# The token part of a decoder layer's projection: plain x against scaled weights, in a front written out as one fixed order

## The chip, the cores and the metric

The kernel runs on one core of a Trainium2 chip. The metric is device time: microseconds (us) from start to end of one execution of the program. Five engines work side by side, each from its own instruction queue: PE (TensorE, the matmuls), ACT (ScalarE), DVE (VectorE), POOL (GpSimd) and SP (SyncE, which here only issues DMAs). They meet at semaphores.

## The reference, cut to what matters

One layer of a decoder trunk for 1024 prompt tokens of one request and 8 x 8 = 64 tokens of eight sample requests, D = 1024, all in float32:

```python
def rms_norm(x, g):
    y = xf * lax.rsqrt(jnp.mean(xf * xf, axis=-1, keepdims=True) + EPS)
    return (y * g.astype(jnp.float32)).astype(x.dtype)
...
mod = (jax.nn.silu(c) @ w_ada + b_ada)[:, None, :]
shift1, scale1, gate1, shift2, scale2, gate2 = jnp.split(mod, 6, axis=-1)
h = rms_norm(x, norm1) * (1 + scale1) + shift1
z = h @ w_in
(q, kc, vc, ks, vs, kw, vw, gates, conv_bg, conv_cg, conv_h, pool_in) = jnp.split(z, IN_SPLITS, axis=-1)
```

`c` differs by request: the prompt has one row of `shift1` and `scale1`, each of the eight sample requests has its own. Then follow attention of three kinds, a short convolution, a pooling, the output projection and a SwiGLU; the change touches none of them. The change concerns `h`, and the 280 columns of `z` that are wanted with the tokens as rows: `vs`, `vw` (128 columns each) and `gates` (24).

## The kernel before, in words

Everything up to `h` is called the front here. Tokens lie in three **chunks** of columns, `CHUNKS = [(0, 384), (384, 384), (768, 320)]`; the last 64 columns of chunk 2 are the sample tokens. A chunk is a tile of 128 partitions x 8 k-tiles x columns, with the channels on the partitions. Chunk 0 is loaded into `x0`, chunk 1 into the memory of `kv`, chunk 2 into `x2`. SP's queue carries x of chunk 0, 16 tiles `wada` of 256 KB (modulation round 1, the scale), x of chunk 1, two halves of the token weights `wtok`, 16 more `wada` (round 0, the shift), x of chunk 2, `w1` of the compression, and then twelve blocks `cacheA`.

- **Modulation** (`ada_rounds`): 16 tiles of weights by the 32 columns of `sc` = silu(c) fill a PSUM bank; ACT copies it out (`ada_s`), PE transposes it (L145), DVE adds the bias (`mod`, L397), and after round 1 forms `s1` = (1 + scale1) * norm1 (L404).
- **Norm** (`norm_scale`): ACT squares x by k-tile (`n_t`, L441), PE multiplies `mean_d` by each square (8 float32 matmuls of 384 columns for each of the chunks 0 and 1; for chunk 2 DVE adds the squares into `n_ss` and one matmul follows), ACT takes the root, DVE the reciprocal of all 384 columns (L448), so `n_rs` holds 1/rms of each token on all partitions.
- **h** (`modulate`): DVE multiplies x by s1 and `n_rs` in place (L468), ACT adds the shift and rounds to the matmul's type (`h_hi`, L475), DVE forms the rest (`h_lo`, L477). Products are made of three matmuls (`mm3`): hi by hi, hi by lo, lo by hi.
- **Token part** (`token_part`): the 280-column weights are split into `wt_hi` (ACT) and `wt_lo` (POOL). For each of nine tiles of 128 tokens, 24 matmuls: the tile of h is stationary, 280 columns of weights move (8 k-tiles x 3 products). ACT or DVE copies the bank into `vt` and `gates`, and POOL's queue stores it. The ninth tile overlaps the eighth and holds the sample tokens. After the sixth (`tok_last`) the compression may begin.
- **Projections**: then `input_projection` multiplies the other column tiles of w_in (kc, vc, cg0, ch0, ...) with weights as the stationary side and h moving, chunk by chunk (24 matmuls of 384 or 320 columns each). Tile kc needs `w_hi`, `w_lo` (128 x 1024, ACT and DVE) and the h of all three chunks.

All of this is written as generators (`front`, `token_part`, `compress`, `first_ahead`, `late_ada`) that a small scheduler interleaves by estimated engine times; what stands in an engine's queue runs in that order. Matmuls all go through one helper, line L141, and so have one line.

## Time and profile before

| | |
|---|---|
| median of 3 runs | 1627.37 us (1626.49 to 1627.93) |
| the profiled execution's own time | 1627.8 us |
| its span | 1626.2 us |
| PE busy | 1554.4 us (96%), 12569 matmuls |
| DVE, ACT, POOL busy | 1026.3, 720.5, 591.8 us |
| mean granted TensorE clock | 0.983 |

The span lies between the first and the last instruction; 1.6 us of the time lie outside it. Busy time counts matmuls, vector and scalar operations, not the issue of DMAs. The idle time before an instruction is put down to what released it last. A PE row of the timeline gives the start, the time to the modelled end of the last matmul in it, the shapes, the count, and the idle time ahead of it. Matmuls overlap, so the price of one in a run is the distance of successive starts, not its duration. Float32 matmuls leave two records for each instruction.

### The profile page before, as it was taken

The numbers are of one execution on the slowest core, as the hardware profiler recorded it, in microseconds if no ns is written. First come the engines' busy times: TensorE is split into PE (matmuls) and PEld (weight loads), VectorE is DVE, ScalarE is ACT, GpSimd is POOL, SyncE is SP. The second block draws the span as 40 slices with busy tenths as digits, with TensorE's granted clock in tenths as the row PEclk, the third lists the DMA queues.
The fourth block names the chain that finished last, engine by engine and source line by source line (L and its number), as shares of the span: only waits on it lengthen the run. The fifth ranks groups of instructions, "written<-read, shape, count | busy, mean of one in ns | idle before, by whom it ended". The sixth has DMA issues, their size and how long they took to land.

```text
span 1626.2 us, 34746 instructions
## 1 busy us (share of the span) xinstructions
PE 1554.4 (96%) x12569; PEld 1378.6 (85%) x12569; DVE 1026.3 (63%) x2474; ACT 720.5 (44%) x1654; POOL 591.8 (36%) x715
## 2 busy tenths in 40 slices
PE   6899999996899999999899999999999999999999
PEld 2899997895776666556599999999999999999999
DVE  4723224896465577756589878776777776257462
ACT  3522215444576776765657544433334334223220
POOL 3241110166333222322212366544454444276140
PEclk9999999998999999999999999999999999999999
DMA  9486655454565575234287775446333445999872
GB/s 339 173 290 195 197 173 165 147 182 148 176 188 158 155 207 181 81 120 138 90 309 235 262 253 182 149 143 211 137 140 141 149 149 189 322 395 345 285 237 85
DMA packets 197597, 318.06 MB, mean 196 GB/s; under 512 B 26353, under 2 KB 130354, under 8 KB 197106
## 3 DMA queue, kind: packets, MB, share of 16 engines
q1 hardware_dynamic: 174930, 277.15, 51.1%
q0 software_dynamic: 9568, 28.40, 5.3%
q10 hardware_dynamic: 12928, 10.29, 2.0%
q8 instruction: 100, 1.64, 0.4%
q14 instruction: 71, 0.58, 0.1%
HBM read 245.75 MB, written 74.20 MB: 197 GB/s over the span
## 4 chain that ended last, share of the span: by engine, by line
PE 44%; DVE 5%; DMA 3%; ACT 3%; issue 3%; POOL 2%; SPq 0%; ACTq 0%; POOLq 0%; DVEq 0%
PE bank L141 43%; ACT P L1148 2%; DMA w_raw<-in_wup 1%; PE bank L145 1%; DVE P L1136 1%; DVE w_lo L173 1%; DMA pair<-mix_d 1%; POOL b_t L173 0%; DVE b_lo L173 0%; ACT w_hi L177 0%; DMA x_d<-x1a 0%; POOL pair L1779 0%; POOL f_T L173 0%; DMA w_raw<-in_wout 0%; DVE co L1458 0%
## 5 line engine op out<-in xcount | busy, mean ns | idle before, releaser
L141 PE MATMUL bank<-b_lo,w_hi 128*128 128x272 f32 x1232 | 352.8, 288 | 1.0 <-DVE b_lo L173 1.0
L141 PE MATMUL bank<-b_hi,w_hi 128*128 128x272 f32 x1232 | 350.5, 289 | 2.4 <-ACT f_m L1752 1.0
L141 PE MATMUL bank<-b_hi,w_lo 128*128 128x272 f32 x1232 | 347.4, 288 | 0.0
L141 PEld LDWEIGHTS bank<-b_hi,w_hi 128*128 128x128 f32 x1232 | 229.8, 188 | 4.9 <-ACT f_m L1752 2.8
L141 PEld LDWEIGHTS bank<-b_lo,w_hi 128*128 128x128 f32 x1232 | 231.6, 188 | 2.0 <-DVE b_lo L173 1.9
L141 PEld LDWEIGHTS bank<-b_hi,w_lo 128*128 128x128 f32 x1232 | 229.5, 188 | 0.0
L1158 POOL TENSOR_SCALAR P<-P,st 128x128 f32<-128x128 f32 (+10 forms) x192 | 108.4, 578 | 227.5 <-DVE st L1154 150.0
L173 DVE TENSOR_TENSOR w_lo<-w_raw,w_hi 128x512 fp32r<-128x512 f32 (+1 forms) x111 | 102.7, 935 | 72.8 <-ACT w_hi L177 72.2
L141 PEld LDWEIGHTS bank<-stream 128*128 128x128 f32 x1056 | 127.2, 198 | 18.1 <-issue 11.3
L141 PE MATMUL bank<-stream 128*128 128x128 f32 x1056 | 133.4, 284 | 7.1 <-DMA stream<-in_cacheA 7.0
L1148 ACT ACTIVATE P<-P,st 128x128 f32<-128x128 f32 (+10 forms) x192 | 112.7, 588 | 52.3 <-DVE st L1136 33.5
L141 PE MATMUL bank<-h_hi,w_hi 128*128 128x384 f32 (+1 forms) x384 | 130.7, 340 | 0.5 <-DVE q L769 0.5
L177 ACT ACTIVATE w_hi<-w_raw 128x512 fp32r<-128x512 f32 (+1 forms) x113 | 75.7, 687 | 123.9 <-PE bank L141 90.4
L141 PE MATMUL bank<-h_hi,w_lo 128*128 128x384 f32 (+1 forms) x384 | 126.3, 329 | 0.0
L141 PE MATMUL bank<-h_lo,w_hi 128*128 128x384 f32 (+1 forms) x384 | 125.6, 327 | 0.0
L173 DVE TENSOR_TENSOR w_lo<-w_s,w_hi 128x512 fp32r<-128x512 f32 x110 | 111.1, 1010 | 15.7 <-ACT w_hi L177 13.1
L141 PE MATMUL bank<-g,w_hi 128*128 128x272 f32 x608 | 114.6, 288 | 0.0
L1779 POOL TENSOR_TENSOR pair<-pair,f_v 128x272 f32<-128x272 f32 x44 | 44.5, 1012 | 186.2 <-DVE f_v L1749 145.5
L173 POOL TENSOR_TENSOR w_s<-w_raw 128x512 f32<-128x512 f32 x60 | 88.4, 1474 | 44.5 <-DVE w_lo L173 42.1
L141 PEld LDWEIGHTS bank<-g,w_hi 128*128 128x128 f32 x608 | 94.9, 188 | 0.0
L177 ACT ACTIVATE w_hi<-w_s 128x512 fp32r<-128x512 f32 x110 | 69.0, 628 | 52.6 <-PE bank L141 30.5
L141 PE MATMUL bank<-g,w_lo 128*128 128x272 f32 x304 | 86.4, 287 | 0.0
(399 smaller groups left out, 3694.6 us busy)
## 6 DMA issues: line engine op xcount, KB each, us to landing
g<-g_d SPq DMA_DIRECT2D x42, 816.0 KB, 6.7
g_d<-f_s SPq DMA_DIRECT2D x57, 544.0 KB, 3.4
wada<-in_wada SPq DMA_DIRECT2D x96, 256.0 KB, 5.2
stream<-in_cacheA SPq DMA_DIRECT2D x192, 128.0 KB, 3.2
unit<-in_cacheB SPq DMA_DIRECT2D x152, 128.0 KB, 2.3
w_raw<-in_wup SPq DMA_DIRECT2D x38, 512.0 KB, 4.3
stream<-in_cacheB SPq DMA_DIRECT2D x104, 128.0 KB, 2.2
w_raw<-in_wout SPq DMA_DIRECT2D x24, 512.0 KB, 5.0
```

Source lines behind the costliest of these rows:

```text
L141: return self.nc.tensor.matmul(out, lhsT, rhs, start=start, stop=stop, skip_group_check=chain)
L145: return self.nc.tensor.transpose(out, in_, self.ident if ident is None else ident)
L173: (self.nc.vector if eng == "dve" else self.nc.gpsimd).tensor_tensor(out, a, b, op=op)
L177: self.last_hi = self.nc.scalar.activation(hi, src, AF.Copy)
L1136: self.last_evac = nc.vector.tensor_tensor_reduce(out=Pt[:, 2 * g + hl, col:col + n], in0=S[g][:, p0:p0 + n], in1=mk, scale=-1.0, scalar=3 ...
L1148: nc.scalar.activation(Ps, Ps, AF.Exp, scale=-1.0, bias=sy[:, g, 0:1], accum_out=sy[:, g, 1:2])
L1158: nc.gpsimd.tensor_scalar(Ps, Ps, sy[:, g, 3:4], 0.0, op0=OP.mult, op1=OP.add)
L1779: nc.gpsimd.tensor_tensor(g[:, 1], s1, v, op=OP.mult)
```

## The change: what it does

Algebra: with r = 1/rms of a token (a row of the token part's result) and s, sh per channel, (x * r * s + sh) @ w = r * (x @ (s * w)) + sh @ w. In the kernel after,

- the token weights are multiplied by s1 (`w[0]` on ACT, `w[1]` on DVE) and x is split without any scaling (`hi`, `lo`); eight token tiles multiply these; ACT applies r when it copies the bank out (`out`), as a number for each partition. The term sh @ w comes from 8 matmuls of 32 columns over the raw weights, a mean matmul, and is added to `vt` and `gates` at the very end of the front, on DVE;
- the sum of squares is added up on DVE, one matmul of a single column for each 128 tokens gives the mean square with the tokens on the partitions (`sums`), the reciprocal is taken of three numbers a partition, and three matmuls by the identity lay it out over the columns again (`spread`) for the final h;
- the sample tokens go another way: x of these 64 columns is scaled and shifted on DVE and multiplied by the raw weights in 8 float32 matmuls with 64 stationary columns;
- the final h (`scaled`, `hi2`, `lo2`) is formed behind: chunk 0 among the last token tiles, chunk 1 after the first `yield`, chunk 2 after the second. The split of kc's weights stands between chunk 0 and chunk 1, that of vc's between 1 and 2;
- everything in the front is issued through `ordered`, which chains the instructions of each engine in the order of the code. `wada` has 12 buffers instead of 16; the last four tiles of round 0 are asked for after the matmuls `ada(4)`. On SP's queue `w1`, kc's and vc's raw weights (which take over the buffers of `wada`) and four `wada` of a later round (in the memory of `x0`) follow, and only then the blocks `cacheA`.

```diff
+    def front(self, h, np_, ap, tp):
...
+        def sums(c):
+            m = self.bank()
+            for q, a in enumerate(starts(c)):
+                M(m[:, q:q + 1], ss[:, a:a + P], self.mean_d[:, 0:1], True, True)
+            A(rt[c], m[:, 0:3], AF.Sqrt, bias=self.eps[:, 0:1])
+            V("reciprocal", rt[c], rt[c])
+            b = np_.tile([P, 384], F32, name="n_rb")
+            V("tensor_copy", b.rearrange("p (q m) -> p q m", q=3), rt[c][:, :, None].to_broadcast([P, 3, P]))
+            return b
...
+        def scaled(c, k):
+            n = size[c]
+            V("scalar_tensor_tensor", x[c][:, k, :n], x[c][:, k, :n], s[:, k, 0:1], rs[c][:, :n], op0=OP.mult, op1=OP.mult)
...
+        def out(j, acc):
+            r = rt[j // 3][:, j % 3:j % 3 + 1]
+            A(self.vt[:, j, 0:256], acc[:, 0:256], AF.Copy, scale=r)
+            A(self.gates[:, j, :], acc[:, 256:280], AF.Copy, scale=r)
...
+        for k in range(KT):
+            square(0, k)
+            hi(0, k)
+            lo(0, k)
...
+        b = sums(0)
+        ada(3, acc)
+        t = ada_rows(acc)
+        ada_turn(t, 1)
...
+        for k in range(KT):
+            A(w[0][:, k], raw[k // 4][:, k % 4], AF.Copy, scale=s[:, k, 0:1])
+            V("scalar_tensor_tensor", w[1][:, k], raw[k // 4][:, k % 4], s[:, k, 0:1], w[0][:, k].bitcast(F32),
+              op0=OP.mult, op1=OP.subtract)
+        spread(0, b)
+        t0 = token(0)
...
+        t3 = token(3)
+        b = sums(1)
+        ss = self.pair384(0)
+        run(square, 2, range(8))
+        acc = self.bank()
+        ada(4, acc)
+        ada_load(7)
+        out(3, t3)
+        ada(5, acc)
+        t4 = token(4)
+        spread(1, b)
+        run(hi, 2, range(8))
+        run(lo, 2, range(8))
+        b = sums(2)
+        ada(6, acc)
+        out(4, t4)
+        ada(7, acc)
+        t = ada_rows(acc)
+        spread(2, b)
+        run(scaled, 0, range(8))
...
+        t5 = token(5)
+        self.tok_last = self.order["pe"]
+        X(self.w1, i["w1"].rearrange("p v k m -> p (v k) m"))
+        ada_turn(t, 0)
...
+        run(hi2, 0, range(8))
+        run(lo2, 0, range(8))
+        t6 = token(6)
+        m = self.bank()
+        for y in range(2):
+            for g in range(4):
+                M(m[32 * g:32 * g + 32, 0:280], sb[:, 4 * y + g], raw[y][:, g], y == 0, y == 1)
+        acc = self.bank()
+        for k in range(KT):
+            M(acc[64:128, 0:280], v[:, k], raw[k // 4][:, k % 4], k == 0, k == KT - 1)
+        t7 = token(7)
+        yield
...
+        M(m[:, 0:280], self.mean_d, part, True, True)
...
+        run(scaled, 1, range(8))
+        run(hi2, 1, range(8))
+        run(lo2, 1, range(8))
+        yield
+        run(scaled, 2, range(8))
...
+        run(hi2, 2, range(8))
+        run(lo2, 2, range(8))
+        for d, a, n in ((self.vt, 0, 256), (self.gates, 256, 24)):
+            V("scalar_tensor_tensor", d[:, 0:8], m[:, None, a:a + n].to_broadcast([P, 8, n]), float(D // 32), d[:, 0:8],
+              op0=OP.mult, op1=OP.add)
```

In `input_projection` the two `yield`s of `front` are met so:

```diff
             load()
             load()
-            split()
+            front_split()
+            next(front)
+            front_split()
+            for _ in front:
+                pass
...
+            self.spawn(0.6, self.up_weights_ahead(pp, 0))
             self.spawn(0.5, self.late_ada())
```

**PE, the start of the program.** Before: `n_t` are the squares of x, `wada,sc` the modulation, `ident,ada_s` its transposes; the first token matmul is the last row shown.

```order
L141 MATMUL bank<-n_t,mean_d 128x384 x3
L141 MATMUL bank<-wada,sc 32x256 x2
L141 MATMUL bank<-n_t,mean_d 128x384 x2
L141 MATMUL bank<-wada,sc 32x256 x6
L141 MATMUL bank<-n_t,mean_d 128x384
...
L141 MATMUL bank<-wada,sc 32x256 x22
L145 MATMUL bank<-ident,ada_s 128x128 x2
L141 MATMUL bank<-wt_hi,h_hi_103 128x280
```

After, from the first matmul on (`pair_182` is the sum of squares of chunk 0, `n_rb` the 1/rms that is laid out; `h_hi_103` holds plain x here):

```order
L141 MATMUL bank<-wada,sc 32x256 x24
L141 MATMUL bank<-mean_d,pair_182 128x1 x3
L141 MATMUL bank<-wada,sc 32x256 x8
L145 MATMUL bank<-ident,ada_s 128x128 x2
L141 MATMUL bank<-ident,n_rb 128x128 x3
L141 MATMUL bank<-wt_hi,h_hi_103 128x280
```

Both modulation rounds and the means of chunks 0 and 1 stood ahead of the first token matmul; now one round and three one-column matmuls do.

**PE, from the fifth token tile to the first projection, after.** The second modulation round, the layouts of chunks 1 and 2, and the matmuls of the shift (`ct`) and of the sample tokens (`x_153`):

```order
L141 MATMUL bank<-ident,n_rb 128x128 x3
L141 MATMUL bank<-mean_d,pair_484 128x1 x3
L141 MATMUL bank<-wada,sc 32x256 x16
L141 MATMUL bank<-ident,n_rb 128x128 x2
L141 MATMUL bank<-ident,n_rb 128x64
...
L141 MATMUL bank<-stream,ct 32x280 x8
L141 MATMUL bank<-stream,x_153 64x280 x8
...
L141 MATMUL bank<-n_t,mean_d 128x280
L141 MATMUL bank<-h_hi_103,w_hi 128x384
```

The first projection (kc, the last row) now follows the mean matmul of the shift; of the compression's matmuls (`c_peT`, `stream 128x128`), which stood among the last token tiles and ahead of kc in the kernel before, none stands ahead of it.

**DVE, the forming of h.** Before (`x_154` is chunk 0, `kv__98` chunk 1, `s_128` is s1, `h_lo_104` and `h_lo_106` the rest of h):

```order
L448 RECIPROCAL n_rs<-n_rs 128x384
L397 TENSOR_TENSOR mod<-bank,c_bada 128x4x9 x2
L404 SCALAR_TENSOR_TENSOR s_128<-mod,c_norm_113 128x72
L468 SCALAR_TENSOR_TENSOR x_154<-x_154,s_128,n_rs 128x384 x8
L448 RECIPROCAL n_rs<-n_rs 128x384
L468 SCALAR_TENSOR_TENSOR kv__98<-kv__98,s_128,n_rs 128x384 x8
L397 TENSOR_TENSOR mod<-bank,c_bada 128x4x9 x2
L477 SCALAR_TENSOR_TENSOR h_lo_104<-x_154,mod,h_hi_103 128x384 x8
```

After, from the rest of plain x of chunk 2 (`h_lo_108`) to the end of the front's work on chunk 1 (`pair_328` and `pair_563` hold 1/rms of chunks 0 and 1, laid out):

```order
L370 TENSOR_TENSOR h_lo_108<-x_153,h_hi_107 128x256 x8
L370 RECIPROCAL n_rt_156<-n_rt_156 128x3
L370 COPY n_rb<-n_rt_156 128x384
L370 SCALAR_TENSOR_TENSOR x_152<-x_152,s_128,pair_328 128x384 x8
...
L370 COPY ct<-mod 128x256
L370 TENSOR_TENSOR x_153<-x_153,mod 128x8x64
L370 SCALAR_TENSOR_TENSOR h_lo_104<-x_152,mod,h_hi_103 128x384 x8
L173 TENSOR_TENSOR w_lo<-w_raw,w_hi 128x1024
L370 SCALAR_TENSOR_TENSOR kv__98<-kv__98,s_128,pair_563 128x384 x8
L370 SCALAR_TENSOR_TENSOR h_lo_106<-kv__98,mod,h_hi_105 128x384 x8
```

The reciprocals of 384 columns are gone; the scaling of x and the forming of `h_lo` stand behind the splits of plain x, and `w_lo` of kc (L173) between chunk 0 and chunk 1.

## Rows read from the trace of the kernel before

**Rows 1.** The page's span and its row of busy times (busy us, share of the span, instructions).

```profile
span 1626.2 us, 34746 instructions
PE 1554.4 (96%) x12569; PEld 1378.6 (85%) x12569; DVE 1026.3 (63%) x2474; ACT 720.5 (44%) x1654; POOL 591.8 (36%) x715
```

**Rows 2.** The windows of core 0: from-to and length in us, then busy us (instructions) of PE, weight loads, DVE, ACT and POOL, the granted clock, the busy share of the DMA engines and GB/s.

```profile
0.00:45.00 45.00, 29.59 (x164) 10.62 (x164) 20.45 (x36) 15.33 (x27) 13.50 (x23) 1.00 0.97 346
45.00:58.20 13.20, 10.29 (x74) 9.87 (x75) 12.06 (x26) 11.42 (x26) 1.62 (x3) 0.95 0.53 166
58.20:88.60 30.40, 30.40 (x242) 30.20 (x241) 19.18 (x41) 12.68 (x27) 11.74 (x18) 0.96 0.52 188
88.60:118.47 29.87, 29.87 (x196) 27.69 (x194) 7.84 (x15) 8.63 (x19) 11.54 (x17) 1.00 0.80 270
...
350.00:850.00 500.00, 455.96 (x4374) 334.09 (x4373) 327.41 (x1291) 314.42 (x842) 163.97 (x288) 0.95 0.53 162
...
0.00:10.00 10.00, 0.00 (x0) 0.00 (x0) 0.55 (x6) 2.13 (x3) 6.32 (x17) 1.00 0.76 235
10.00:20.00 10.00, 9.86 (x42) 3.27 (x42) 1.09 (x6) 2.60 (x6) 0.00 (x0) 1.00 1.05 380
```

**Rows 3.** The three longest waits of PE up to 90 us: what was waited for, us in total, times, the longest.

```profile
PE bank L141 <- ACT n_t L441: 10.4, 2, 10.1
PE bank L141 <- DVE n_ss L173: 2.9, 1, 2.9
PE bank L141 <- ACT h_hi L475: 2.3, 1, 2.3
```

**Rows 4.** The timeline of PE, from the last token tile to the second projection's end (start, us, engine, line, matmul, shapes, count). At 88.60 kc begins, at 118.47 cg0.

```profile
79.08 3.63 PE L141 MATMUL bank<-c_peT,stream 128*128 128x2 f32 x32
82.57 6.27 PE L141 MATMUL bank<-stream 128*128 128x128 f32 x54
88.60 0.42 PE L141 MATMUL bank<-h_hi,w_hi 128*128 128x384 f32 x1
...
118.47 0.42 PE L141 MATMUL bank<-h_hi,w_hi 128*128 128x384 f32 x1
```

**Rows 5.** The loads at the start: SP's issue of the 16 `wada` of round 1, and ACT's first work on x, with its wait.

```profile
2.10 13.66 SPq L368 DMA_DIRECT2D wada<-in_wada  x16
...
9.57 0.52 ACT L441 ACTIVATE n_t<-x 128x384 f32<-128x384 f32 x1 [5.99 <-DMA x<-in_xT]
```

**Rows 6.** The timelines of ACT and DVE: the split of kc's weights (`w_hi`, `w_lo`), the forming of s1 (`s<-mod`), and the scaling of chunk 2's 256 prompt columns.

```profile
28.23 2.60 DVE L404 SCALAR_TENSOR_TENSOR s<-mod,c_norm 128x72 f32<-128x72 f32 x1
...
62.27 3.25 DVE L468 SCALAR_TENSOR_TENSOR x<-x,s,n_rs 128x256 f32<-128x256 f32 x8
...
78.54 1.04 ACT L177 ACTIVATE w_hi<-w_raw 128x1024 fp32r<-128x1024 f32 x1
...
79.61 1.23 DVE L173 TENSOR_TENSOR w_lo<-w_raw,w_hi 128x1024 fp32r<-128x1024 f32 x1
```

**Rows 7.** The timeline of PE at the front: modulation matmuls, transposes, and the token matmuls at either clock.

```profile
10.14 1.65 PE L141 MATMUL bank<-n_t,mean_d 128*128 128x384 f32 x2 [10.14 <-ACT n_t L441]
...
17.47 0.91 PE L141 MATMUL bank<-n_t,mean_d 128*128 128x384 f32 x2
...
26.71 1.56 PE L141 MATMUL bank<-n_t,mean_d 128*128 128x384 f32 x4
...
36.10 1.93 PE L141 MATMUL bank<-wada,sc 128*32 128x256 f32 x30
...
45.01 0.40 PE L141 MATMUL bank<-wt_hi,h_hi 128*128 128x280 f32 x1 [2.31 <-ACT h_hi L475]
...
57.44 1.43 PE L141 MATMUL bank<-n_ss,mean_d 128*128 128x320 f32 x2 [2.90 <-DVE n_ss L173]
...
58.90 0.43 PE L141 MATMUL bank<-wt_lo,h_hi 128*128 128x280 f32 x1
59.13 0.43 PE L141 MATMUL bank<-wt_hi,h_lo 128*128 128x280 f32 x1
...
60.48 0.29 PE L141 MATMUL bank<-wt_hi,h_lo 128*128 128x280 f32 x1
...
60.99 0.29 PE L141 MATMUL bank<-wt_hi,h_hi 128*128 128x280 f32 x1
```

**Rows 8.** Page, DMA issues: KB each and median us from issue to landing.

```profile
wada<-in_wada SPq DMA_DIRECT2D x96, 256.0 KB, 5.2
stream<-in_cacheA SPq DMA_DIRECT2D x192, 128.0 KB, 3.2
```

**Rows 9.** Groups by shape over the whole span (busy us, mean ns of one, idle before): the nearest form to the sample matmuls (64 stationary columns).

```profile
L141 PE MATMUL bank<-pair,c_w 64*64 64x256 f32 x64 | 7.7, 433 | 3.9 <-ACT pair L625 3.9
```

**Rows 10.** The timeline of DVE: the scaling of chunk 0, eight operations that begin while POOL works on the token weights, and the same eight of chunk 1.

```profile
30.86 6.51 DVE L468 SCALAR_TENSOR_TENSOR x<-x,s,n_rs 128x384 f32<-128x384 f32 x8
...
39.88 4.32 DVE L468 SCALAR_TENSOR_TENSOR kv__98<-kv__98,s,n_rs 128x384 f32<-128x384 f32 x8
```

**Rows 11.** The timeline of POOL: the two operations of the token weights, then issues of DMAs.

```profile
28.18 5.09 POOL L173 TENSOR_TENSOR wt_lo<-stream,wt_hi 128x1120 fp32r<-128x1120 f32 x2 [18.85 <-ACT wt_hi L177]
33.21 2.15 POOL L533 DMA_DIRECT2D stream<-in_cacheA  x4
```

**Rows 12.** The waits of PE over the whole span: the blocks of the compression.

```profile
PE bank L141 <- DMA stream<-in_cacheA: 7.0, 3, 5.0
```

More of the change, by code (lines that the diff above doesn't have):

```diff
@@ L546, in compress @@
         yield from self.hold(lambda: self.tok_last)
-        if self.w1 is None:
+        if not self.compressing:
+            self.compressing = True
+            yield from self.hold(lambda: self.w_load)
             yield from self.compress_setup(pool)
@@ L683, in load @@
             if i < len(srcs):
+                if i == 0:
+                    st["hi"] = pool.tile([P, D], F32R, name="w_hi", bufs=bufs)
                 t = pool.tile([P, D], F32, name="w_raw", bufs=raw_bufs)
-                nc.sync.dma_start(t, srcs[i])
+                load_ = nc.sync.dma_start(t, srcs[i])
+                if i < 2:
+                    self.w_load = load_
                 st["raw"][i] = (t, self.use("dma", 1.45, self.t["pe"]) + 2.0)
@@ L694, in split @@
                 t, at = st["raw"].pop(i)
-                hi = pool.tile([P, D], F32R, name="w_hi", bufs=bufs)
+                hi = st["hi"] if i == 0 else pool.tile([P, D], F32R, name="w_hi", bufs=bufs)
                 lo = pool.tile([P, D], F32R, name="w_lo", bufs=bufs)
@@ L716, in project @@
         return acc[:, :n]
-    def token_loads(self):
-        for half in range(2):
-            raw = self.stream_tile().rearrange("p a b -> p (a b)")[:, 0:1120].rearrange("p (k m) -> p k m", k=4)
-            self.nc.sync.dma_start(raw, self.i["wtok"][:, half * 4:half * 4 + 4])
-            self.wt_raw.append((raw, self.use("dma", 1.5, self.t["pe"]) + 2.0))
-    def token_part(self, pool, h):
-        nc = self.nc
-        hi = pool.tile([P, KT, 280], F32R, name="wt_hi")
-        lo = pool.tile([P, KT, 280], F32R, name="wt_lo")
-        yield from self.hold(lambda: self.wt_raw)
-        for half, (raw, at) in enumerate(self.wt_raw):
-            s = slice(half * 4, half * 4 + 4)
-            yield at
-            r = self.split(hi[:, s], lo[:, s], raw, 1120, at, "pool")
-        yield r
-        for j in range(9):
-            c0 = j * P if j < 8 else T - P
-            ch = next(k for k, (a, n) in enumerate(CHUNKS) if a <= c0 and c0 + P <= a + n)
-            yield from self.hold(lambda: ch in self.h_done)
-            yield max(self.h_at[ch])
-            s = slice(c0 - CHUNKS[ch][0], c0 - CHUNKS[ch][0] + P)
-            acc = self.bank()
-            for k in range(KT):
-                last = self.mm3(acc[:, :280], (h[ch][0][:, k, s], h[ch][1][:, k, s]), (hi[:, k], lo[:, k]),
-                                k == 0, k == KT - 1)
-            if j == 5:
-                self.tok_last = last
-            self.evac(self.vt[:, j, 0:256], acc[:, 0:256], 256)
-            nc.vector.tensor_copy(self.gates[:, j, :], acc[:, 256:280])
-            self.use("dve", 0.1)
-            nc.gpsimd.dma_start(self.o["vtok"][j], self.vt[:, j, 0:256])
-            yield 0.0
-        nc.scalar.activation(self.gates, self.gates, AF.Sigmoid)
-        self.use("act", 0.4, table="sigmoid")
     def head_norm(self, pool, out, acc, n, gain, tag="b", done=None):
@@ L895, in input_projection @@
         self.vcp = zp.tile([64, P], F32, name="vcp")
-        self.spawn(0.6, self.first_ahead())
-        with self.pool("tok", "left") as tp:
-            yield from self.token_part(tp, h)
-        yield from self.hold(lambda: self.ahead)
-        hn_, hn, pp_ = self.ahead
+        nc.gpsimd.memset(self.gates[0:64, 8], 0.0)
+        norm_, ada_, tok_ = self.pool("norm"), self.pool("ada"), self.pool("tok", "left")
+        front = self.front(h, norm_.__enter__(), ada_.__enter__(), tok_.__enter__())
+        next(front)
+        ada_.__exit__(None, None, None)
+        tok_.__exit__(None, None, None)
+        nc.vector.tensor_scalar(self.qgain, self.qgain_raw, 0.125, None, op0=OP.mult)
+        self.t.update(pe=56.0, act=58.0, dve=64.0, pool=50.0, dma=45.0)
+        self.h_at = [[50.0] * KT, [60.0] * KT, [66.0] * KT]
         zq_ = self.pool("zq", "left")
@@ L925, in tiles @@
                         self.z_steps += 1
-                        if ch == 0:
+                        if ch == 0 and nm != "kc":
                             split()
@@ L1020, in load @@
                 W[i] = tiles, self.use("dma", 2.9, self.t["pe"]) + 5.5
+        rows = [pool.tile([P, 256], F32, name="ada_s")]
         load(0)
@@ L1035, in late_ada @@
             for h in range(2):
-                s = pool.tile([P, 256], F32, name="ada_s")
+                s = rows.pop() if rows else pool.tile([P, 256], F32, name="ada_s")
                 r_ = self.evac(s, acc[:, 256 * h:256 * h + 256], 256)
```

328 lines of the change are left out of this document (160 added, 168 removed).

## Prediction

> **What bounds the kernel now.** The page comes first: PE is busy for 1554.4 of the 1626.2 us of the span [rows 1], so only what PE executes, or waits for, can move the time. The windows say where it waits: between 0 and 45 us it is busy for 29.59, between 45 and 58.2 for 10.29 of 13.20; from 58.2 to 118.47 it has no gap; the next large ones (44 us) lie between 350 and 850 [rows 2], behind the change. The front's waits have names: 10.1 us for the first squares (that is, for x), 2.3 for the first `h_hi`, 2.9 for the sum of squares of chunk 2 [rows 3]. Between them PE does work that the change removes: seventeen mean matmuls of whole chunks, and the ninth token tile.
>
> So I measure the front by one point, kc's first matmul, at 88.60 before. The compression's matmuls ahead of it, 3.5 us of `c_peT` and 6.0 of `stream` from 79.08 to 88.60 [rows 4], and ten more `stream` records among the token tiles (1.1 by the same spacing), stand behind kc's first two chunks in the kernel after; they are moved, not removed. Like for like, kc begins at 88.6 − 10.6 = 78.0. From there to cg0 (118.47) PE is busy without a gap [rows 2, 4], and the same matmuls follow in the kernel after.
>
> **The change, step by step, on PE.**
>
> (1) The first modulation round ends PE's wait for data. x of chunk 0 (1.57 MB), 16 `wada` (4.19) and `cT` (0.13) are 5.9 MB; the queues move 2.35 MB in the first 10 us and 380 GB/s then [rows 2], which gives 19.3. By these two rates x and `cT` (1.7 MB) were through between 7.2 and 8.3, and the first square began at 9.57 [rows 5]: data are used 1.3 to 2.4 later than that count, I take 1.5: 20.8. The squares and splits of chunk 0 (about .5 us each) keep pace on ACT and DVE. The last modulation matmuls take .6: 21.4.
>
> (2) Copy and transposes .9, two adds .3, s1 .2, first `wt_hi` .4, three handovers of .15: 23.6. The row of s1 shows 2.60, not .2 [rows 6], but for 72 columns, and while POOL splits the token weights, which the change removes.
>
> (3) Tokens 0 to 3: 96 matmuls at .128 (60.48 to 60.99 is four steps [rows 7]), 12.3 us. Weights come from DVE at some .45 a k-tile (by width from .41 for 256 columns [rows 6]), token 0 uses one in .38: +.5. The clock is unknown here. Before, PE started at the lower level: a pair of `n_t` records took 1.65 until 17.47 and .91 from then on [rows 7], 7.3 us at half speed, 3.7 lost. After, that stretch is bound by transfers; but PE waits about 2 us ahead of token 0. After the wait of 2.31 at 45.01 it kept the upper level; after that of 2.90 at 57.44 it fell: matmuls .235 apart at 58.90, .128 from 60.48 on [rows 7]. The bounds are 0 and 3.7; I take 2.0. This ends at 38.4.
>
> [...]
>
> (4) To the end of `spread(2)`. PE has `sums(1)` .7 (three matmuls of one column at the .22 of `c_peT`'s, 3.5 us for 32 records, two for each [rows 4]), sixteen modulation matmuls at .13 (1.93 us for 30 records [rows 7]) 2.1, token 4 3.1, a spread .7: 6.6. Then it waits for DVE: copy of 1/rms .5, first `hi` .4, eight `lo` of 256 columns 3.3 (3.25 for eight [rows 6]), reciprocal and copy .5, handovers .6: 5.3, of which `sums(2)` and the sixteen matmuls of the round's second half fill 2.8. With the last spread, .7, that is 38.4 + 12.6 = 51.0, PE idle for about 2.5 of it. The last `wada` are asked for after `ada(4)`, some 8 us before their use; a `wada` needs 5.2 to land [rows 8]: hidden by 3.
>
> (5) Token 5 3.1, transposes .5, token 6 3.1, the shift's eight matmuls 1.05, the sample tile 8 × .36 = 2.9, token 7 3.1, mean matmul .6: 14.3. No trace row has the sample tile's form: 64 stationary columns with 256 moving took .24 (7.7 us for 64 records, two each [rows 9]), the full width .65 for 384 columns (1.56 less .91 [rows 7]), .47 for 280; I take the middle, .36. For the clock +.7 (0, and 1.5 as at 57.44). kc begins at **66.0**, 12.0 earlier than like for like.
>
> **What must be in time.** Kc's raw weights are asked for as the second round's buffers come free, by 50, and take as long as a `wada` or a little more: there by 57. DVE is the engine late next. From 51 on it scales chunk 0 (4.3), handles the samples (2), forms `h_lo` 0 (4.3): with what PE's transposes release, 61.0. `w_hi` of kc waits for that: 62.2, `w_lo` (1.23 [rows 6]) 63.6, so kc at 66.0 has 2.4 to spare. Scaling and `h_lo` of chunk 1 end at 72.2, and PE, after kc's chunk 0 (4.2) and a moved modulation group (1.0), wants the first k-tile of chunk 1 at 71.2, with each later one .53 on: DVE is ahead by about 2.8. w_lo of vc 73.5, chunk 2 80.7; PE wants it after vc's chunk 0, at 81.8. On SP's queue late `wada` loads wait for x0's memory, that is for the last `h_lo` 0, and behind them stand the blocks `cacheA` and vc's successors: the first octet lands at about 71.9 (landing 3.2 [rows 8]), wanted at 73.8. Not one of these has more than 3 us, and I keep a reserve of 2.0 for handovers and short stalls that this count doesn't see (0 to 5).
>
> **Sum.** 12.0 − 2.0 = 10.0 us gained: 1627.8 − 10.0 = **1617.8**. 1627.8 is the profiled execution's own time, 1.6 above its span and .4 above the median; I don't correct for .4. All terms at their good ends (clock 0 and 0, sample tile .25, no reserve) gain 15.6: 1612.2. All at their bad ends (3.7, 1.5, .47, reserve 5) gain 12.0 − 1.7 − .8 − .9 − 3.0 = 5.6; with the first loads at the 346 GB/s of the first 45 us [rows 2] in place of 380 after 10 us, .9 less: 4.7, 1623.1.
>
> **Rivals.**
>
> *The clock stays low (no change), .07.* For it: the waits ahead of token 0 and at 57.44. Against it: the recovery after three microseconds at 60.48. [...]
>
> *DVE becomes the bound (slower), .07.* Between 38 and 81 us DVE has some 66 operations with two inputs, nearly without a break. Eight of these took 6.51 us beside POOL's work, against 4.32 without [rows 10]: .27 more each. At that pace 66 cost 18 us, less 2 of slack: 1617.8 + 16 = 1633.8. It decides where POOL's work coincides: 37 of the 66 at that pace take back the gain, 49 make it slower by more than 0.2%. Against it: POOL's work beside them was the two `wt_lo`, 5.09 us, which are gone; its issues of DMAs from 33.21 to 35.36 [rows 11] did not lengthen DVE's operations beside them; in the front after, POOL issues little and computes nothing.
>
> [...]
>
> *Given back later (hardly any gain), .08.* What is earlier at cg0 may be lost in the waits between 350 and 850, if these hang on transfers: PE waited for the compression's blocks for 7.0 us in all [rows 12], and these are now asked for later. If 7 of the 10 go so: 1624.8. Against it: most of those waits are for ACT and DVE inside the attention, which move along.
>
> *More than all good ends, .06*: DVE's chain bounds it, about 1611.
>
> *Likeliest, .72*: a gain as summed, its own range 1612.2 to 1623.1. The range 1612.0 to 1625.0 holds it with most of the third rival. Three runs can tell about 0.2%, 3.3 us. Faster by more: .72 + .06 + half of the third, .82; within: .07 and the other half, .11; slower: .07.
>
> **What would show it.** Right: the first token matmul at 23 to 25 instead of 45.01; the second round's last spread at about 51; kc's first matmul at 64 to 69; between it and cg0 no wait of PE over 1 us; the waits behind 350 unchanged. Wrong: token matmuls .235 apart for more than 4 us; a wait of PE for `h_lo`, `w_lo` or `cacheA` near kc of several us; DVE's two-input operations of 384 columns above .54 apart; a later stage longer by microseconds.

## The result, and the profile after

Five executions of the changed kernel have a median of 1619.25 us (1613.58 to 1620.88), five of the kernel before beside them 1627.93. The ratio is 0.9938, with a 95% interval of 0.9917 to 0.9958: some 10 us, or 0.6%, faster (the two medians are 8.7 us apart, the two profiled executions 7.9). In two later groups of runs, shown below, the ratio was 0.9941 (0.9928 to 0.9954) and 0.9925 (0.9911 to 0.9939). The forecast was 1617.8 from 1627.8, a gain of 10.0 us, range 1612.0 to 1625.0.

The profiled execution of the changed kernel took 1619.91 us, 1.6 of them outside its span. Its page:

```profile
span 1618.3 us, 34879 instructions
PE 1550.7 (96%) x12581; PEld 1379.1 (85%) x12581; DVE 1037.4 (64%) x2517; ACT 732.5 (45%) x1697; POOL 582.6 (36%) x707
```

Against [rows 1] the span is 7.9 us shorter, and PE's busy time only 3.7: half of the gain is waiting that is gone, half is work. The waits of PE in the first 120 us of the changed kernel (us in total, times, longest):

```profile
PE bank L141 <- DMA wada<-in_wada: 13.1, 2, 10.9
PE bank L145 <- ACT ada_s L369: 0.6, 1, 0.6
PE bank L141 <- ACT wt_hi L369: 0.6, 1, 0.6
PE bank L141 <- DVE wt_lo L370: 0.2, 1, 0.2
```

The wait for x at the start is about as long as before, only under another name (10.9 for the first `wada`, which ride behind x). The waits for `h_hi` and `n_ss` of [rows 3] don't exist any more; a new one of 2.18 us, for the last `wada`, has come. In the two later profiles of the same kernel it was .90 and .28. PE's timeline of the changed kernel (start, us, tiles, shapes, records, idle before):

```profile
10.88 8.60 PE L141 MATMUL bank<-wada,sc 128*32 128x256 f32 x48 [10.88 <-DMA wada<-in_wada]
...
20.17 1.90 PE L141 MATMUL bank<-wada,sc 128*32 128x256 f32 x16
...
24.26 0.39 PE L141 MATMUL bank<-wt_hi,h_hi 128*128 128x280 f32 x1 [0.55 <-ACT wt_hi L369]
...
37.61 0.80 PE L141 MATMUL bank<-mean_d,pair 128*128 128x1 f32 x6
...
48.40 1.05 PE L141 MATMUL bank<-wada,sc 128*32 128x256 f32 x10 [2.18 <-DMA wada<-in_wada]
49.38 1.07 PE L141 MATMUL bank<-ident,n_rb 128*128 128x128 f32 x6
...
56.97 1.15 PE L141 MATMUL bank<-stream,ct 128*32 128x280 f32 x16
58.05 3.99 PE L141 MATMUL bank<-stream,x 128*64 128x280 f32 x16
...
61.97 0.40 PE L141 MATMUL bank<-wt_hi,h_hi 128*128 128x280 f32 x1
...
65.42 0.54 PE L141 MATMUL bank<-h_hi,w_hi 128*128 128x384 f32 x1
...
85.35 4.44 PE L141 MATMUL bank<-c_peT,stream 128*128 128x2 f32 x32
...
97.92 0.42 PE L141 MATMUL bank<-h_hi,w_hi 128*128 128x384 f32 x1
```

The first token matmul stands at 24.26 (45.01 before, [rows 7]), the fourth tile's end at 37.6, the second round's last layout at 49.38 to 50.45, kc's first matmul at 65.42. That is 12.6 us earlier than the 78.0 which the prediction took as like for like. The last two rows are the block of two-column matmuls of the compression, which stood ahead of kc before, and the next projection matmul behind the compression's first share. DVE keeps its pace in the new front (.54 for each operation of 384 columns), and w_lo of kc ends 3.5 us ahead of PE's need:

```profile
48.52 4.31 DVE L370 SCALAR_TENSOR_TENSOR x<-x,s,pair 128x384 f32<-128x384 f32 x8
...
54.40 0.29 DVE L370 COPY ct<-mod 128x256 f32<-128x256 f32 x1
...
55.22 4.32 DVE L370 SCALAR_TENSOR_TENSOR h_lo<-x,mod,h_hi 128x384 fp32r<-128x384 f32 x8
60.65 1.23 DVE L173 TENSOR_TENSOR w_lo<-w_raw,w_hi 128x1024 fp32r<-128x1024 f32 x1 [1.12 <-ACT w_hi L177]
```

**Where the 12.6 went.** Three instructions that both kernels have show how much of the lead is left at a place. On DVE's timeline of before (the last is the last of the program):

```profile
157.89 0.28 DVE L804 SCALAR_TENSOR_TENSOR cy<-us,c_convw,cy 128x64 f32<-128x64 f32 x1
...
303.99 0.17 DVE L872 COPY pe_x<-pe_f 64x16 f32<-64x16 f32 x1
...
1622.63 0.50 DVE L1888 SCALAR_TENSOR_TENSOR x<-bank,mod,x 128x272 f32<-128x272 f32 x1 [3.63 <-PE bank L141]
```

and the same in the changed kernel, with one row more at 294:

```profile
148.59 0.28 DVE L881 SCALAR_TENSOR_TENSOR cy<-us,c_convw,cy 128x64 f32<-128x64 f32 x1
...
294.19 1.41 DVE L948 SCALAR_TENSOR_TENSOR pe_x<-pe_s,pe_x 64x1208 f32<-64x1208 f32 x1 [1.22 <-DMA out_poolS<-pe_x]
...
295.84 0.17 DVE L949 COPY pe_x<-pe_f 64x16 f32<-64x16 f32 x1
...
1614.75 0.50 DVE L1980 SCALAR_TENSOR_TENSOR x<-bank,mod,x 128x272 f32<-128x272 f32 x1 [3.63 <-PE bank L141]
```

9.3 us are left at 158, 8.15 at 304 (DVE waited 1.22 for a store to be done with its tile; the two later profiles of this kernel have no such wait at that row), 7.9 at the end. So 3.3 of the 12.6 are lost behind kc, ahead of 158. The windows of the changed kernel there (busy us and counts of PE, weight loads, DVE, ACT, POOL; granted clock; DMA share; GB/s):

```profile
85.00:88.00 3.00, 3.00 (x29) 3.00 (x27) 1.86 (x4) 2.95 (x7) 0.01 (x1) 0.99 0.53 183
88.00:91.00 3.00, 3.00 (x15) 3.00 (x15) 1.47 (x8) 0.03 (x1) 2.91 (x4) 0.50 0.80 253
91.00:94.00 3.00, 3.00 (x15) 1.11 (x13) 0.42 (x1) 0.42 (x1) 0.72 (x1) 0.50 0.95 320
94.00:97.00 3.00, 3.00 (x24) 3.00 (x25) 0.38 (x1) 0.56 (x2) 2.73 (x5) 0.87 0.83 234
```

PE is busy all the time, but its granted clock is at the lower level, 0.50, from about 88 to 95. What it worked on when the clock fell was the block of sixteen two-column matmuls of the compression (`c_peT`, from 85.35 on), then 128-column and 512-column ones at about half speed (ten records of the first took 2.41 us at 89.65, 32 took 3.49 at 116.90 in the run `after_same_chip` below; a group of the second took 1.86 at 92.06, and .99 at 107.48 there). Before, the same block stood at 79.08 [rows 4] and the clock stayed up, at 1.00 from 79 to 88.6. The rows give the price: from the first 128-column matmul to the projection matmul at 97.92 PE needed 8.27 us, and 5.88 for the same in the run `no_peT` below, where the clock stayed up; the block itself took 4.30, and 3.49 in the next run. Together that is 3.2, nearly all of the 3.3.

### The profile page after: what moved, and what is told of

It is laid out like the page before. It is cut to its first block, busy times and chain, and to the rows that moved or that the text cites. A ratio compares the mean times of both kernels' runs of the same rounds, so it can differ in the third digit from the quotient of the medians.

```text
span 1618.3 us, 34879 instructions
## 1 busy us (share of the span) xinstructions
PE 1550.7 (96%) x12581; PEld 1379.1 (85%) x12581; DVE 1037.4 (64%) x2517; ACT 732.5 (45%) x1697; POOL 582.6 (36%) x707
## 4 chain that ended last, share of the span: by engine, by line
PE 44%; DVE 5%; issue 3%; ACT 2%; DMA 2%; POOL 2%; ACTq 0%; POOLq 0%; DVEq 0%
PE bank L141 43%; ACT P L1237 2%; PE bank L145 1%; DVE P L1225 1%; DVE w_lo L173 1%; DMA pair<-mix_d 1%; DMA w_raw<-in_wup 1%; POOL b_t L173 0%; DVE b_lo L173 0%; ACT w_hi L177 0%; DVE x1a L1606 0%; POOL pair L1871 0%; POOL f_T L173 0%; DVE f_s L173 0%; DMA w_raw<-in_wout 0%
## 5 line engine op out<-in xcount | busy, mean ns | idle before, releaser
L173 DVE TENSOR_TENSOR w_lo<-w_raw,w_hi 128x512 fp32r<-128x512 f32 (+1 forms) x111 | 103.0, 937 | 65.7 <-ACT w_hi L177 64.0
L173 DVE TENSOR_TENSOR w_lo<-w_s,w_hi 128x512 fp32r<-128x512 f32 x110 | 110.5, 1005 | 15.7 <-ACT w_hi L177 12.7
L173 POOL TENSOR_TENSOR w_s<-w_raw 128x512 f32<-128x512 f32 x60 | 87.3, 1455 | 44.3 <-DVE w_lo L173 42.1
L641 POOL DMA_DIRECT2D stream<-in_cacheA x64 | 35.4, 554 | 163.2 <-PE bank L141 120.7
```

Of the source, the lines that this page charges most:

```text
L173: self.last_lo = (self.nc.vector if eng == "dve" else self.nc.gpsimd).tensor_tensor(out, a, b, op=op)
L641: eng.dma_start(dst[:, a + j, :], self.i[name][bass.ds(regs[j], 1)].rearrange("n p f -> (n p) f"))
```

## The experiments

**Base, and a block moved.** The changed kernel once more, and a version that spreads the `c_peT` matmuls over the eighth token tile (cut: the block at its old place goes, and the copy of its result moves with it):

```diff
-        t7 = token(7)
+        t7, pe = self.bank(), self.bank()
+        for k in range(KT):
+            token(7, [k], t7)
+            for n in (2 * k, 2 * k + 1):
+                M(pe[:, n // KT * 2:n // KT * 2 + 2], self.w1[:, n], self.pe[:, n // KT, n % KT, :], n % KT == 0, n % KT == KT - 1)
```

> The changed kernel once more, on the chip of the three that follow, as their base. Theory A: the granted clock falls to its lower level behind kc and vc, when PE works on the two-column matmuls of the compression (c_peT), in nearly every execution, and costs 3.3 us there (the gain was 12.6 us at kc's first matmul and 9.2 at 114 us); then this profile shows a half-clock stretch of about 7 us near 88 again, and the time is 1619 to 1620. Rival B: the fall is chance, part of the kernel's scatter of 7 us between executions (1613.6 to 1620.9); then the stretch can be missing here, and the time of an execution without it is 1616 or less.

> The sixteen two-column matmuls of the compression are moved out of their block behind vc into the eighth token tile, two behind each of its k-tiles, between dense matmuls; nothing else is changed. Theory A (the block of narrow matmuls lowers the clock): kc begins 3.5 us later (69 instead of 65.4), no half-clock stretch between 60 and 120 us, and the time is 3.3 us below the changed kernel. Rival B (the fall near 88 is chance): the clock falls there or elsewhere as often as before, no difference beyond 1 us. Rival C (mixing narrow with dense matmuls lowers the clock for the dense too): token matmuls .235 apart in the eighth tile, 3 us slower.

Measured: 1616.87 us (1614.6 to 1618.09), ratio 0.9941 (0.9928 to 0.9954), for the changed kernel; 1616.28 (1613.23 to 1619.91), ratio 0.9937 (0.9922 to 0.9953), for the other. In the base kc began at 65.10 and the lower clock was there again, 0.50 from 89.5 on, this time half as long (3.4 us for 6.8). With the matmuls spread, kc began at 68.18 and the stretch is gone:

```profile
88.00:91.00 3.00, 3.00 (x28) 3.00 (x28) 1.90 (x4) 2.98 (x7) 1.17 (x3) 1.00 0.66 208
91.00:94.00 3.00, 3.00 (x27) 2.04 (x26) 1.05 (x4) 0.55 (x2) 2.81 (x4) 1.00 0.95 307
```

Theory A is right on the clock and wrong on the time: nothing is gained that these runs can tell. The scheduler sets the order behind the front anew when the block is absent. PE's timeline of the late modulation groups in that version (eight records are one group):

```profile
109.59 1.06 PE L141 MATMUL bank<-wada,sc 128*32 128x512 f32 x6
...
111.55 1.05 PE L141 MATMUL bank<-wada,sc 128*32 128x512 f32 x2 [0.90 <-DMA wada<-in_wada]
...
124.01 1.05 PE L141 MATMUL bank<-wada,sc 128*32 128x512 f32 x4
...
125.72 1.05 PE L141 MATMUL bank<-wada,sc 128*32 128x512 f32 x2
...
127.59 1.05 PE L141 MATMUL bank<-wada,sc 128*32 128x512 f32 x2
```

and in the base:

```profile
107.48 1.06 PE L141 MATMUL bank<-wada,sc 128*32 128x512 f32 x8
...
124.09 1.11 PE L141 MATMUL bank<-wada,sc 128*32 128x512 f32 x8
```

One group now comes to its weights too early (a wait of .90), and the next is cut in three by projection matmuls: each piece, of four or two records, took .97 or .98 as far as the matmul behind it, where the whole group took 1.05 in the base. From kc's first matmul to the start of the modulation group at 184.60 in the base (187.54 here), both have the same other matmuls, and the rows add up to the same: 119.50 and 119.36 us. Saved are 3.5 for the block and .9 on the 128-column matmuls that had run at half clock. Lost are 2.1 in the seven modulation groups (9.95 for 7.89), .9 in the wait, .8 among the projection matmuls and .6 at a group of 64-column ones. As kc itself began 3.1 later, because the block now stands ahead of it, the version is 2.9 behind there.

**The block left out, and the block in a wait.** The first leaves out fourteen of the sixteen matmuls (`for k in (KT - 1,)` in the block's loop, so its result is incomplete), the second puts all of them where PE waited for the last `wada` and takes the block away from its old place (cut):

```diff
+        X(self.w1, i["w1"].rearrange("p v k m -> p (v k) m"))
         t3 = token(3)
...
         ada(6, acc)
         out(4, t4)
+        pe = self.bank()
+        for n in range(16):
+            M(pe[:, n // KT * 2:n // KT * 2 + 2], self.w1[:, n], ...)
         ada(7, acc)
```

> Leaves out fourteen of the sixteen two-column matmuls (the positional part of the compression is then incomplete). Theory A (PE sets the pace behind kc, the half-clock stretch near 88 is due to these matmuls): no half clock between 60 and 120 us, 3.1 us of matmuls and 1.7 to 3.4 of clock fall away, the time is 4.5 to 6.5 below the changed kernel. Rival B (the transfers behind kc, 322 GB/s at .95 busy from 88 to 123, set the pace as soon as PE gets ahead): PE waits for wada or cacheA there, and less than 3 us are gained.

> The changed kernel as the base for the next one, on the same chip: by the executions so far 1614 to 1621, ratio to the kernel before .994. In three of three profiles with the block of two-column matmuls behind kc a half-clock stretch of 3.4 to 6.8 us began at 88 to 89.5; theory A expects it a fourth time.

> w1 is asked for ahead of the second round's last four tiles, and the sixteen two-column matmuls stand where PE waited 2.2 us for these tiles, between the third and the last quarter of the round. Theory A: they cost 1.3 us there instead of 3.5 and the 1.7 to 3.4 us of half clock behind kc go, so kc begins 1.3 us later (66.5) and what follows is 3 to 5 us earlier; of that 40% were given back in the run without these matmuls (4.6 at 100 us, 3.1 at 150, 2 at the end), so 2 us below the changed kernel at the end. Rival B: narrow matmuls behind a short wait lower the clock at 46 to 50, where tokens 5 and 6 pay up to 3.4 us: no gain. Rival C: w1 ahead of the four tiles delays them, PE waits longer: no gain.

Measured: without them 1614.15 us (1612.04 to 1614.82), ratio 0.9927 (0.9901 to 0.9953), kc at 65.24, the clock at the upper level up to 360 us (1.00 from 85 to 94), and no wait of PE between 66 and 130. By the ratios that is 0 to 2 us below the changed kernel (0.9941 and 0.9925 in the two bases), but the interval is 4 us wide on either side, so the times decide nothing between theory A's 4.5 to 6.5 and rival B's less than 3. The profile does. PE is at the projection matmul that stood at 97.92 in the changed kernel here:

```profile
91.41 0.42 PE L141 MATMUL bank<-h_hi,w_hi 128*128 128x384 f32 x1
```

6.5 earlier, .2 of it at kc. That is close to theory A's 6.5 for a stretch as long as this, and PE waited for no transfer, so rival B's cause is absent. By the modulation group at 181.51 (186.52 there) 5.0 of it are left. What becomes of the rest shows beside the other profiles; the table has the lead over the one profile of the kernel before, in us, at the second and the third of its rows of DVE above:

| profile | kc | lead at 304 | lead at the end |
|---|---|---|---|
| changed kernel | 65.42 | 8.15 | 7.9 |
| `after_same_chip` | 65.10 | 11.25 | 13.2 |
| `after_same_chip2` | 65.42 | 9.4 | 11.7 |
| `peT_in_front` | 68.18 | 8.3 | 10.2 |
| `no_peT` | 65.24 | 14.35 | 13.1 |

At 304 the run without the block leads each profile of the changed kernel by 3.1 to 6.2 us. Behind 304, where none of these edits reaches, the lead still moves by −1.3 to +2.3 from one profile to the next, and what the front gave can drown in that. Why it moves there was not taken apart.

The base of the second run: 1614.96 (1612.12 to 1617.63), ratio 0.9925 (0.9911 to 0.9939), kc at 65.42, the lower clock from 87.7 on, as theory A expected. In the wait, 1619.43 (1618.0 to 1622.73), ratio 0.995 (0.9937 to 0.9964): 4 us slower than its base. kc began at 67.78, not 66.5:

```profile
45.50 3.73 PE L141 MATMUL bank<-c_peT,stream 128*128 128x2 f32 x32
49.16 1.93 PE L141 MATMUL bank<-wada,sc 128*32 128x256 f32 x16
```

The block filled the wait and outlasted it, 3.7 us for the 1.3 that I had left over, and the clock fell at 49.2, right behind it (sixteen `wada` records in 1.93, and in 1.07 at 40.67 of the run `ada4_early` below): rival B in its result, though PE no longer waited there.

Over all ten profiles with the block in one piece (before, the changed kernel three times, and six variants), the granted clock fell in or right behind the block in eight, for 3.4 or 6.8 us (to 0.50, for 6.8, 3.4 and 6.8, in the three of the changed kernel); it did not in the kernel before and in the variant with more DVE work. In the two without it, there was no fall between 60 and 360 us (means of 1.00 from 69 to 125 and from 125 to 350 in `peT_in_front`, and 1.00 from 85 to 94 in `no_peT`). The block stood at 45.5, at 85, and at 91 to 105 in these eight, and the fall moved with it. So the fall goes with the block, but it doesn't come each time. One of the eight is less sure: at 45.5 to 49.2 in `peT_in_wait`, since the variant with more DVE work shows a fall at 48.4 without the block, behind the wait. Falls elsewhere, behind waits of PE, are not counted here.

**The last `wada` asked for earlier.**

```diff
+        acc = self.bank()
+        ada(4, acc)
+        ada_load(7)
         t3 = token(3)
         b = sums(1)
...
-        acc = self.bank()
-        ada(4, acc)
-        ada_load(7)
```

> The first quarter of the second modulation round, and with it the request for the round's last four tiles, stands ahead of the fourth token tile instead of behind it. In the changed kernel PE waited 2.18 us for these tiles at 48.40, which the prediction had called hidden by 3. Theory A (the request is late by its place): the wait goes. But the second layout that follows needs DVE's copy of 1/rms, ready at 48.6, and began at 49.38: so kc comes only 0.7 to 0.9 us earlier, and the time falls by as much. Rival B: the transfer is late because the queue is full; the wait stays at 1.5 or more and nothing changes. Rival C: the whole 2.2 us are gained.

Measured: 1616.89 us (1614.8 to 1618.78), ratio 0.9939 (0.9926 to 0.9952): no change. The wait for the tiles went, and another took its place, on PE ahead of the layout:

```profile
50.23 1.04 PE L141 MATMUL bank<-ident,n_rb 128*128 128x128 f32 x6 [1.53 <-DVE n_rb L370]
```

kc began at 66.25, later by 1. The matmuls that moved ahead of the fourth token tile pushed that tile, the sums behind it, and so DVE's chain of squares, splits and reciprocals: all of theories A to C had left this out. Of the 2.18 us hardly any were to be had: DVE's copy of 1/rms ended at 48.6, and in the two bases, where the wait was only .90 and .28, kc began at 65.10 and 65.42, as with 2.18.

**One part undone: the second modulation round ahead of the tokens** (cut: the same calls go from their old places).

```diff
         spread(0, b)
+        acc = self.bank()
+        ada(4, acc)
+        ada_load(7)
+        ada(5, acc)
+        ada(6, acc)
+        ada(7, acc)
+        t = ada_rows(acc)
+        ada_turn(t, 0)
         t0 = token(0)
...
```

> Undoes one part of the change: the second modulation round (16 tiles of 256 KB, its matmuls, transposes and adds) stands ahead of the first token matmul again, as in the kernel before; scaled weights, plain x and the late forming of h stay. Theory A (the gain comes from what tokens need not wait for): 4.2 MB at 380 GB/s put the first token matmul from 24.3 to about 35, PE's 2.1 us of matmuls and its wait of 2.2 us go from behind, so kc begins at about 72 (65.4 in the changed kernel), and the time is about 6.5 us above the changed kernel, still 1 to 3 below the kernel before. Rival B (the gain comes from the fewer and narrower matmuls and the shorter reciprocals): less than 2 us above the changed kernel.

Measured: 1636.53 us (1635.56 to 1637.86), ratio 1.006 (1.0045 to 1.0074): 1.2% above the changed kernel, and slower than the kernel before. PE's timeline:

```profile
32.90 7.37 PE L141 MATMUL bank<-wada,sc 128*32 128x256 f32 x38 [8.89 <-DMA wada<-in_wada]
...
45.09 0.38 PE L141 MATMUL bank<-wt_hi,h_hi 128*128 128x280 f32 x1
...
85.14 0.55 PE L141 MATMUL bank<-h_hi,w_hi 128*128 128x384 f32 x1
```

The first token matmul is back at 45.09, as in the kernel before, and kc at 85.14: 20 us later, and 20 us it is at the end. Theory A holds in kind, at three times its 6.5 us; rival B, that the fewer matmuls and the shorter reciprocals are what gains, is out. My 35 for the first token matmul had left out that x of chunks 1 and 2 and the token weights (4.0 MB) are ahead of that round in SP's queue. That the tokens need not wait for the shift is the change's whole gain and more. With the wait back, the new front is dearer than the old: 40.05 us from the first token matmul to kc, against 33.0 before, like for like. Of these 7, 4.7 are two waits for DVE that neither kernel has:

```profile
PE bank L141 <- DVE n_rb L370: 3.3, 1, 3.3
PE bank L141 <- DVE pair L370: 1.4, 1, 1.4
```

and the granted clock was at its lower level from 64.6 to 71.5, behind and in these waits.

**One part alone: the sums on DVE, in the kernel before** (`if True:` for `if c == 2:` in `norm_scale`; the tile `n_t` of squares also has two buffers in place of three).

> The kernel before with one part of the change alone: the squares of chunks 0 and 1 are added up on DVE and one mean matmul of 384 columns follows, instead of eight; nothing else. Theory A (the first token matmul waits for the second modulation round, not for PE's mean matmuls): the first token matmul stays at 45 (44 to 46), the time within 1 us of the kernel before, although 15 of PE's busy time in the front are gone. Rival B (the mean matmuls crowd PE in the front): 3 us or more faster.

Measured: 1640.58 us (1640.26 to 1641.07), ratio 1.0095 (1.007 to 1.012). Neither theory: the first token matmul moved to 60.98. The longest of PE's waits up to 130 us:

```profile
PE bank L141 <- DVE n_ss L173: 21.5, 3, 16.4
```

The scheduler put the mean matmul of chunk 2 ahead of the token tiles, and PE's queue stood behind it for 16.4 us. So this says nothing on the mean matmuls by themselves; it shows what one row at a wrong place of PE's queue can cost. A share of it is clock, which was at the lower level from 47.9 to 65.0 (token matmuls .23 apart from 61.68 to 62.84).

**DVE's slack, and POOL beside DVE.** Sixteen operations more on DVE; twelve on POOL at the same place:

```diff
         spread(2, b)
+        t_ = work()
+        for k in range(16):
+            V("scalar_tensor_tensor", t_, x[0][:, k % 8, :384], s[:, k % 8, 0:1], rs[0][:, :384], op0=OP.mult, op1=OP.mult)
         run(scaled, 0, range(8))
```

```diff
         spread(2, b)
+        t_ = work()
+        for k in range(12):
+            nc.gpsimd.tensor_tensor(t_, raw[k % 2].rearrange("p k m -> p (k m)")[:, 0:384], b, op=OP.mult)
         run(scaled, 0, range(8))
```

> The changed kernel with sixteen operations more on DVE (the form of the scaling, 384 columns, .54 us each, 8.6 in all; what they compute isn't used) behind the second round's last layout, ahead of the scaling of chunk 0. Theory A (DVE is the engine late next, as predicted): kc's w_lo ended at 61.9 and the rest of h of chunk 1 was ready 3.6 us ahead of PE in the changed kernel, so 3.5 of the 8.6 are hidden: kc begins at 70.3 to 70.7 (65.1 to 65.4 in the changed kernel), PE waits some 5 us in front of it for w_lo, and the time is 4 to 5.5 us above the changed kernel. Rival B (PE is not near DVE's chain; handovers on ACT and the transfers behind kc set the time): under 2 us more.

> The changed kernel with twelve operations on POOL that it does not need (384 columns, two inputs in SBUF, some .9 us each by the width of the 2.55 us for 1120 columns, about 11 us) from the third copy of 1/rms on, beside DVE's scaling and forming of h of chunk 0. Tests the rival that named DVE's slower pace, and its price. Theory A (POOL's work and DVE's two-input operations keep each other waiting, as the rows of before suggest: 5.1 us of POOL's work cost DVE 4.6): DVE's sixteen operations of chunk 0 take up to 10 us longer together, kc begins 4 to 7 us later, the time is as much above the changed kernel. Rival B (what was slow in the kernel before was something else): .54 apart as without, kc at 65 to 66, no change.

Measured, more DVE work: 1626.64 us (1622.54 to 1631.2), ratio 1.0008 (0.9993 to 1.0023), the gain gone. The operations took 10.42, not 8.6 (.65 apart; why was not looked into); kc began at 75.19, 9.8 later. PE's wait has another name than I had expected:

```profile
PE bank L141 <- DVE ct L370: 4.9, 1, 4.9
```

`ct`, the shift in the form that its eight matmuls want, is DVE's first debt to PE, and it had 2.3 us to spare (ready at 54.7, used at 56.97), not the 3.5 of w_lo. It came at 64.7, 10.0 later, so 7.7 of the delay are DVE's. The wait shows only 4.9 of them because the clock had fallen at 48.4 and PE itself was late. A second fall at 62.0, in the wait, made the shift's and the sample tile's matmuls 2.0 us longer. Together that is the 9.8, to a tenth. Theory A in kind, at twice its 4 to 5.5 us, with the wrong debt and without the clock.

Measured, POOL beside DVE: 1622.8 us (1619.37 to 1623.34), ratio 0.9979 (0.9967 to 0.999), kc at 72.47, 7.1 later. DVE's timeline:

```profile
49.11 9.58 DVE L370 SCALAR_TENSOR_TENSOR x<-x,s,pair 128x384 f32<-128x384 f32 x8
58.61 1.48 DVE L370 TENSOR_TENSOR x<-x,pair 128x512 f32<-128x512 f32 x1
...
63.02 5.81 DVE L370 SCALAR_TENSOR_TENSOR h_lo<-x,mod,h_hi 128x384 fp32r<-128x384 f32 x8
```

and POOL's:

```profile
49.34 15.89 POOL L554 TENSOR_TENSOR n_t<-stream,n_rb 128x384 f32<-128x384 f32 x12 [40.28 <-ACT ada_s L369]
```

PE paid for it at the shift:

```profile
PE bank L141 <- DVE ct L370: 5.6, 1, 5.6
```

and 1.5 more behind that wait, where the clock was at its lower level from 62.2 to 65.7. The eight scalings took 9.58 instead of 4.31, the samples' product 1.48 instead of .68, `h_lo` 5.81 instead of 4.32, and POOL 15.89 instead of some 11 by my estimate: theory A. Beside POOL's work each of the eight scalings took 1.20 in place of .54. What the second rival was built on is there, at a price above the .27 that I had given it (.66 for each of the eight); in the changed kernel POOL has nothing to do there (busy for 0.00 us from 24 to 60), and the rival doesn't come. The .27 was a mean that hid its source: of the eight operations of [rows 10], seven were as short as ever, .60 by the row below, and one, the first, took 2.81, or 2.2 more; it ran beside the second of POOL's two, which ended at 33.27 [rows 11] (shortest, middle and longest in ns):

```profile
L468 DVE SCALAR_TENSOR_TENSOR x<-x,s,n_rs x8: 604/604/2810, 30.9 to 36.8; 128x384 f32<-128x384 f32 x8
```

## Why the prediction was right, step by step

- **(1), (2) data and first token matmul**: 21.4 and 23.6 forecast, 22.1 (20.17 + 1.90) and 24.26 measured. Both .7 late, by the transfers. s1 took .23 without POOL beside it, as taken. The .15 for a handover was an estimate that no row shows; here `wt_hi` began .04 behind s1, and the first transpose .14 behind ACT's copy. `round0_first` shows that this step is where the gain is.
- **(3) tokens 0 to 3**: end at 38.4 forecast, 37.6 measured, in spite of the later start: 13.35 us in place of 14.8. The 2.0 for the clock was not needed: no half-clock row between 24 and 85, and a granted clock of 1.00 in that stretch. Its bound of 3.7 had been read from the pace of the first matmuls of before; the granted clock of that stretch stands at 1.00 in [rows 2], so the lower level there was inferred and not read. The wait of 2.18 at 46 did not lower the clock here either (1.00 from 42 to 54); in `dve_16_more` it fell at 48.4, behind the same wait of 2.19.
- **(4) second round**: 51.0 forecast, 50.45 measured. The total was right, a part of it wrong: I had PE wait for DVE, with the last `wada` hidden by 3 us; it waited 2.18 for them. The last request left SP at 41.85 (20.16 + 21.69 in the row below), and 6.5 us later the tiles had just come: 5.2 from issue to landing is a median over the program [rows 8], too short for this place. Since DVE's copy of 1/rms was ready at 48.6, the wait cost less than 1 us, which `ada4_early` and the two bases bear out. SP's timeline of the changed kernel:

```profile
20.16 21.69 SPq L372 DMA_DIRECT2D wada<-in_wada  x16
```

- **(5) to kc**: 14.3 + .7 forecast, 14.97 measured. The shift's matmuls took 1.08 (1.05). The sample tile took 3.92, .49 for each of its matmuls: above .36, and a little over the upper bound of .47, so that 64 stationary columns in place of 128 brought nothing here. The clock term of .7, for which there was no half clock, made good for most of it by luck.
- **What must be in time**: DVE came 1.2 to 1.7 us earlier than forecast all along (w_lo at 61.9 for 63.6, vc's at 72.3 for 73.5), no wait for `cacheA`. The first debt was misnamed: it is `ct` with 2.3 to spare, not w_lo with 2.4. (The forecast's terms from 51 to the end of `h_lo` 0 add up to 61.6, not 61.0, so its own slack was 1.8.)
- **The reserve** of 2.0 was meant for handovers near kc; there none was needed. It went into what the sum did not see: the lower clock behind kc, 3.2 us in the profiled execution, 1.6 in another, and 1.2 at a store in the profiled one alone. That the same matmuls, moved, would be paid for at half clock is the step that was missing: the prediction had them moved at their old price. So the mechanism up to kc is right, and that the total came near is in part luck: in the profiled execution 12.6 less 4.7 lost is 7.9, against 12.0 less 2.0 forecast, and a reserve put up for other things covered less than half of the loss.
- **The range's ends**: the bad end was added up wrongly. With the reserve at 5 the sum is 12.0 − 1.7 − .8 − .9 − 5.0 = 3.6, not 5.6 (3.0 is only the reserve's excess over 2.0), and with the slower loads 2.7, or 1625.1 us, just outside the stated range. The measured time needs none of this. In the second rival, 37 and 49 operations leave out the slack of 2; with it they are 44 and 57.
- **The rivals**: the clock through tokens 0 to 4 did not stay low, it was granted at 1.00 (by an estimate from the two paces of [rows 7], .235 and .128, the 120 matmuls of these five tiles would have cost 12.8 us in place of the 2.0 taken); DVE's slower pace did not come, for the reason given; a part was given back, but at 88 to 95 and at 294, not between 350 and 850. The waits behind 350 moved along: PE was busy for 456.78 us there, 455.96 before [rows 2], and waited 6.5 for the compression's blocks, 7.0 before [rows 12].

Left open: why the clock fell behind the block in eight profiles and not in two, and why the lead moves by up to 2.3 us behind 304 from one execution to the next.

## What to carry to other kernels

Scaling that depends on a late value can often be taken out of the operand and applied to the result: what counted here was less the work saved than which transfer the first matmul then waits for (20 us here between the two orders, the waits that came with the other one included). When the front gets shorter, look at what the same matmuls meet at their new place: here sixteen of two columns in a block were followed by a granted clock of 0.50 in all three profiles of the changed kernel. And a wait that the profile names is worth only the distance to the next engine's chain behind it: removing 2.18 us of it gave nothing here.

## What the runs showed of the hardware

- Sixteen matmuls of two columns in one block were followed by a fall of the granted clock in eight of ten profiles, to 0.50 for 6.8, 3.4 and 6.8 us in the three of the changed kernel, where PE was busy throughout (3.00 us of each 3.00 from 85 to 97 in the first of them); spread two at a time between dense ones, by none, in one profile (1.00 from 85 to 97).
- A POOL operation of 384 columns and two inputs that ran beside DVE's took 1.32 us on average (15.89 for twelve), and DVE's two-input operations of 384 columns 1.20 (9.58 for eight) in place of .54.
- A float32 matmul of 280 moving columns with 64 stationary ones took .49 us, about what the full width would take: .47, an estimate by width from .65 for 384 columns in rows of before.
